# A DRAM buffer between two steps of a delta rule, laid out for its reader instead of its writer

## The chip, the cores and the metric

The kernel runs on one core of a Trainium2 chip. The metric is the device time of one execution in microseconds (us); of several runs the median is taken. Five engines work side by side: TensorE (PE in the profile, its weight loads PEld), VectorE (DVE), ScalarE (ACT), GpSimd (POOL) and SyncE (SP). SP does no arithmetic; it issues most of the DMA transfers, one after the other, and an instruction on it that waits holds back those behind it. Each engine works through its own instructions in a fixed order and waits on semaphores for the others. The data of a transfer is moved by 16 DMA engines.

## The reference

One layer of a hybrid block: an input projection feeds two branches, which are gated, projected and merged. Branch A is a gated delta rule in both directions, branch B a differential softmax attention. Sizes: 1024 latent tokens and 256 context tokens, width 1024, 8 heads of 128, all in float32. The change concerns branch A alone, and of it the inverse of a triangular matrix for each chunk of 64 tokens:

```python
a_mat = jnp.where(strict, jnp.einsum('nbhid,nbhjd->nbhij', kc * bc[..., None], kc) * decay, 0.0)
eye = jnp.eye(CHUNK, dtype=a_mat.dtype)
t_mat = lax.linalg.triangular_solve(eye + a_mat, jnp.broadcast_to(eye, a_mat.shape),
                                    left_side=True, lower=True)
u = t_mat @ (vc * bc[..., None])
w = t_mat @ (kc * (bc * jnp.exp(gc))[..., None])
```

`t_mat` feeds a scan over the chunks, one after the other, in each of the two directions. There are 1280 / 64 = 20 chunks in each direction; the kernel treats two chunks as one unit of 128 tokens and so has 10 units (NT) for each direction.

## The kernel before, in words

**Stages.** A front part normalises the tokens and computes the modulation; the input projection follows, in several parts; then comes the delta rule of the 8 heads, mixed with the rest of the projection as filling for TensorE; then the attention, mixed with the first part of the output projection; last `phase3` (from L1728), the rest of the output projections.

**What sets the order.** In the delta rule and the attention the order is planned by hand-written code. Each piece of work is a generator that yields tuples of engine, expected duration, what it depends on, and what to emit; `flow` and `turn_flow` (L70, L95) always take the next step that by these expected times can begin first, with a small handicap for each stream. The result is one fixed order for PE, DVE, ACT, POOL and SP. The expected durations stand in the source, such as 0.91 for the write and 1.82 for the read that the change touches. Outside these sections, in `phase3` too, the tile framework puts the instructions in order by itself, from estimated times of the whole program.

**The inverse of one head** (`gdn_prep`, L973 to L1132) goes by blocks of 32 x 32. A unit of 128 tokens has four diagonal blocks m = 0 to 3; with 10 units in two directions there are 2 * NT = 20 of them, u, and so 80 blocks, each with rows i and columns j.

1. TensorE forms the gram matrices, DVE scales them into `X` (L1018 to L1023). The diagonal blocks go to the DRAM buffer `da`: four transfers of the forward direction (L1034), and for the backward direction one from the tile `cb` (L1037), after a transpose on DVE.
2. *Substitution.* The 80 blocks are loaded into the tile `ab`, one block on each of 80 partitions (L1043). GpSimd clears the tile `ts` and sets its diagonal to one (L1041, L1042); `ab` and `ts` exist once, so each head uses the same ones. DVE then eliminates row by row with 31 pairs of instructions (L1048, L1050).
3. *Through DRAM.* `ts` is written to the buffer `db` (L1052), and `db` is read into `R`, one half of the tile `RR` (L1057), this time with the four blocks of a unit below each other on 128 partitions: partition 32 m + i, then the unit u and column j. The read waits on SP until the write has landed.
4. *Merge.* DVE transposes all blocks (L1058); `placed` copies blocks back into `X` on ACT (L1140) and DVE (L1139) and into `t64` (L1143), and small matmuls `pz`, `p2`, `p3` join the blocks of 32 to blocks of 64 and then 128. The result is written to `xd` (L1129).

**What else stands near it.** The scans (`scan`, L1183) load chunks of `xd` and of the masked products `qkd` (L1176); GpSimd applies the triangular mask (L1178). When a head's scan is over, `tails` normalises its output (L1280), multiplies on GpSimd (L1283), and transposes on TensorE (tile `oT`). Weights of the filling work are split in a high and a low part: ACT casts (`wh`, L765), GpSimd or DVE subtracts (`wl`, L766).

**The last stage.** `phase3` loads the eight heads' attention output `y` (L1761) through two buffers, casts each on ACT (`yh`, L1764) and subtracts on GpSimd or DVE (`yl`, L1765). A buffer is free for the next load when its `yl` is done. The weights are loaded and split in the same manner (L1725, then `wh` L1719 and `wl` L1720), and the matmuls `m` need both.

Of the kernel before, what the change touches and what calls it, by code (L numbers as in the profile page):

```python
# [8 lines left out]
F32 = mybir.dt.float32  # L9
# [14 lines left out]
NT = LT // P  # L24
NL = L // P
H = 8
# [8 lines left out]
PE, DVE, ACT, POOL, DMA, ADMA, DV2, PL1 = range(8)  # L35
# [8 lines left out]
class Block:  # L44
# [143 lines left out]
    def setup(self):  # L188
        nc, a = self.nc, self.a
        cp = self.cp = self.pool("const")  # L190
        self.dp = self.pool("spill", space=DRAM)
        ct = cp.tile([P, 3, P], F32, name="ct")
        nc.sync.dma_start(ct, a["consts"].rearrange("(a p) n -> p a n", p=P))
        self.ident, self.up, self.lo = (ct[:, i, :] for i in range(3))
        self.one = self.lo[:, 0:1]
        self.fold = cp.tile([P, P], F32, name="fold")
        nc.vector.tensor_reduce(self.fold[:, :32], self.ident.rearrange("p (a i) -> p i a", i=32), AX.X, ALU.add)
        for m in range(1, 4):
            nc.vector.tensor_copy(self.fold[:, 32 * m:32 * m + 32], self.fold[:, :32])
        self.mhalf = cp.tile([P, 1], F32, name="mhalf")  # L200
        nc.gpsimd.memset(self.mhalf, -0.5)
        self.da = self.dp.tile([H, 2 * NT, 4, 32, 32], F32, name="da")
        self.db = self.dp.tile([H, 2 * NT, 4, 32, 32], F32, name="db")
        self.ya = self.dp.tile([2, H, P, L], F32, name="ya")
        self.yb = self.dp.tile([H, P, L], F32, name="yb")
        self.gk = self.dp.tile([H, P, LT], F32, name="gk")
        self.gkk = self.dp.tile([H, P, LT], F32, name="gkk")
        self.gv = self.dp.tile([H, LT, P], F32, name="gv")
        self.gkr = self.dp.tile([H, LT, P], F32, name="gkr")
        self.rkd = self.dp.tile([H, LT], F32, name="rkd")  # L210
        self.gq = self.dp.tile([H, P, L], F32, name="gq")
        self.sza = self.dp.tile([H, P, L], F32, name="sza")
        self.szb = self.dp.tile([H, P, L], F32, name="szb")
        self.qd = self.dp.tile([2, H, P, L], F32, name="qd")
        self.kd = self.dp.tile([2, H, P, LT], F32, name="kd")
        self.vd = self.dp.tile([2, LT, H * P], F32, name="vd")
        self.gt = self.dp.tile([2 * KT, P, L], F32, name="gt")
        self.ma = self.dp.tile([KT, P, L], F32, name="ma")
        self.xd = self.dp.tile([H, P, 2, NT, P], F32, name="xd")
        self.qkd = self.dp.tile([H, P, 2, NL, P], F32, name="qkd")  # L220
        self.tbd = self.dp.tile([P, 1024], F32, name="tbd")
        self.gcd = self.dp.tile([2 * H, LT], F32, name="gcd")
        self.gad = self.dp.tile([1, D], F32, name="gad")
        self.rbd = self.dp.tile([H, L], F32, name="rbd")
        for n in ("gk", "gkk", "gv", "gq", "sza", "szb", "qd", "kd", "vd", "gt", "gcd", "ya", "yb"):
            self.dbg[n] = getattr(self, n).name
# [745 lines left out]
    def gdn_prep(self, h):  # L972
        nc, PT, V = self.nc, self.gt_, self.nc.vector  # L973
# [21 lines left out]
        for d in range(2):  # L995
            for c in range(NT):
                t = yield ACT, 0.293, [ld[d]], lambda: nc.scalar.activation(
                    X[:, d, c], X[:, d, c], AF.Abs, bias=self.gcc[:, c, d * H + h:d * H + h + 1], scale=-1.0)
# [5 lines left out]
        for c0 in range(0, NT, 2):  # L1004
# [3 lines left out]
            for j in range(2):  # L1008
                c = c0 + j
                kc = kT[:, c * P:(c + 1) * P]  # L1010
                t = yield PE, 0.2235, [tk, b], lambda: self.mm(pt[:, j * 256:j * 256 + P], kc, kc)
                if c < NL:
                    t = yield PE, 0.2235, [tk, tq, b], lambda: self.mm(pt[:, j * 256 + P:j * 256 + 256], kc, qT[:, c * P:(c + 1) * P])
# [11 lines left out]
            if c0 < NL:  # L1025
                t = yield DMA, 0.91, tQ[-2:], lambda: nc.sync.dma_start(self.qkd[h][:, :, c0:c0 + 2], qk[:, c0 // 2 % 2])
# [13 lines left out]
        ab, ts = T("ab", [80, 32, 32]), T("ts", [80, 32, 32])  # L1040
        t1 = yield PL1, 0.89, [], lambda: nc.gpsimd.memset(ts, 0.0)  # L1041
        t1 = yield PL1, 0.06, [t1], lambda: nc.gpsimd.memset(ts.rearrange("p a b -> p (a b)")[:, 0:1024:33], 1.0)  # L1042
        t = yield DMA, 0.91, st, lambda: nc.sync.dma_start(ab, self.da[h].rearrange("u m i j -> (u m) i j"))  # L1043
        tmp = T("tmp", [80, 256])
        for j in range(31):
            n, w = 31 - j, j + 1
            tv = tmp[:, :n * w].rearrange("p (a b) -> p a b", b=w)
            t = yield DV2, n * w / 960.0 + 0.08, [t, t1], lambda: V.tensor_tensor(  # L1048
                tv, ab[:, j + 1:, j:j + 1].to_broadcast([80, n, w]), ts[:, j, :w].unsqueeze(1).to_broadcast([80, n, w]), ALU.mult)
            t = yield DV2, n * w / 960.0 + 0.08, [t, t1], lambda: V.tensor_tensor(ts[:, j + 1:, :w], ts[:, j + 1:, :w], tv,  # L1050
                                                                               ALU.subtract)
        t = yield DMA, 0.91, [t], lambda: nc.sync.dma_start(self.db[h].rearrange("u m i j -> (u m) i j"), ts)  # L1052
        self.subst = h + 1
        yield lambda: self.merge == h
        RR = T("RR", [P, 2, 2 * NT, 32])
        R, Rt = RR[:, 0], RR[:, 1]
        tR = yield DMA, 1.82, [t], lambda: nc.sync.dma_start(R, self.db[h].rearrange("u m i j -> (m i) u j"))  # L1057
        tt = yield DVE, 0.735, [tR], lambda: V.transpose(Rt, R)  # L1058
        t64, tZ, placed = self.t64, [], []
        self.asides.append(self.placed(X, R, Rt, tt, tZ, placed))  # L1060
# [5 lines left out]
        for c in range(NT):  # L1066
            for (b1, b2) in ((0, 1), (2, 3)):
                t = yield PE, 0.03, [tt, b], lambda: self.mm(pz[B(b1), c], X[B(b2), 0, c, B(b1)], Rt[B(b2), c]), 0.25
                t = yield PE, 0.03, [tt, b], lambda: self.mm(pz[B(b2), c], X[B(b1), 1, c, B(b2)], R[B(b1), NT + c]), 0.25
# [7 lines left out]
        for c in range(NT):  # L1077
            for (b1, b2) in ((0, 1), (2, 3)):
                t = yield PE, 0.03, [tz, b], lambda: self.mm(p2[B(b1), c], R[B(b1), c], Z[B(b1), c]), 0.25
                t = yield PE, 0.03, [tz, b], lambda: self.mm(p2[B(b2), c], Rt[B(b2), NT + c], Z[B(b2), c]), 0.25  # L1080
# [20 lines left out]
        for c0, nb in ((5, 5), (0, 5)):  # L1101
# [4 lines left out]
            for j in range(nb):  # L1106
                c = c0 + j
                t = yield PE, 0.065, [tx, b], lambda: self.mm(pz[lo, j], X[hi, 0, c, lo], X[hi, 0, c, hi]), 0.5
                t = yield PE, 0.065, [tx, b], lambda: self.mm(pz[hi, j], X[lo, 1, c, hi], X[lo, 1, c, lo]), 0.5
# [5 lines left out]
            for j in range(nb):  # L1115
                c = c0 + j
                t = yield PE, 0.065, [tz, t6, b], lambda: self.mm(pu[lo, j], t64[lo, c], Z6[lo, c]), 0.5
                t = yield PE, 0.065, [tz, t6, b], lambda: self.mm(pu[hi, j], t64[hi, c], Z6[hi, c]), 0.5
# [5 lines left out]
            for d in range(2):  # L1124
                for c in range(c0, c0 + nb):
                    t = yield ACT, 0.263, [e, f], lambda: nc.scalar.activation(
                        X[:, d, c], X[:, d, c], AF.Copy, scale=self.beta[:, c, d * H + h:d * H + h + 1])
# [744 lines left out]
```

## Time and profile before

| | |
|---|---|
| median of 3 runs | 2076.24 us |
| runs | 2072.71, 2076.24, 2086.58 us |
| profiled execution | 2065.07 us |
| its span (first to last instruction) | 2063.3 us |
| granted TensorE clock, mean | 0.986 of full speed |
| busy: PE, DVE, ACT, POOL | 96%, 69%, 52%, 38% of the span |
| mean DMA rate | 171 GB/s |

A row of the timeline gives start and duration in us, the engine (a q behind it means its sequencer, here the issue of a transfer), the line, the operation, and out<-in by the tiles' names; in brackets stands how long the engine was idle before it, and who ended that. A row of the windows gives the stretch, its length, the busy time of PE, PEld, DVE, ACT and POOL with the number of instructions, the granted clock, the share of the 16 DMA engines that was busy, and GB/s. A row of the view of one tile gives the count, and the smallest, median and largest duration in ns. The duration of a transfer on SP is that of its issue, not of the movement; when it has landed is seen from the instruction that waits for it.

### The profile page before, as it was taken

The numbers are of one execution on the slowest core, as the hardware profiler recorded it, in microseconds if no ns is written. First come the engines' busy times: TensorE is split into PE (matmuls) and PEld (weight loads), VectorE is DVE, ScalarE is ACT, GpSimd is POOL, SyncE is SP. The second block draws the span as 40 slices with busy tenths as digits, with TensorE's granted clock in tenths as the row PEclk, the third lists the DMA queues.
The fourth block names the chain that finished last, engine by engine and source line by source line (L and its number), as shares of the span: only waits on it lengthen the run. The fifth ranks groups of instructions, "written<-read, shape, count | busy, mean of one in ns | idle before, by whom it ended". The sixth has DMA issues, their size and how long they took to land.

```text
span 2063.3 us, 38606 instructions
## 1 busy us (share of the span) xinstructions
PE 1974.1 (96%) x14207; PEld 1725.9 (84%) x14207; DVE 1423.1 (69%) x3582; ACT 1070.9 (52%) x2328; POOL 774.8 (38%) x644
## 2 busy tenths in 40 slices
PE   8999898899999999999999999999899999998999
PEld 3888677798999997887787888887788888876899
DVE  4797668866876885765665786237679899874532
ACT  4444344354234462566456654547668888773210
POOL 1213224214441331323333323334566667564122
PEclk9999999999999999999999999999999999999999
DMA  9455557545446566557754865648665575335452
GB/s 314 118 148 149 146 141 199 138 163 161 147 136 193 164 203 184 172 178 234 214 196 144 261 182 159 219 144 237 153 174 144 165 200 152 102 109 189 150 158 87
DMA packets 395840, 352.24 MB, mean 171 GB/s; under 512 B 145423, under 2 KB 344689, under 8 KB 395651
## 3 DMA queue, kind: packets, MB, share of 16 engines
q1 hardware_dynamic: 345443, 302.58, 49.9%
q10 hardware_dynamic: 50208, 47.19, 7.5%
q8 instruction: 112, 1.84, 0.4%
q14 instruction: 77, 0.63, 0.1%
HBM read 232.63 MB, written 117.08 MB: 169 GB/s over the span
## 4 chain that ended last, share of the span: by engine, by line
PE 52%; DMA 10%; DVE 8%; ACT 6%; issue 2%; SPq 1%; POOL 1%; ACTq 0%; DVEq 0%; POOLq 0%
PE mm L55 22%; PE chain L55 5%; PE mo L55 4%; PE s L55 3%; PE m L55 3%; PE v L55 3%; DVE S L1453 3%; PE ma L55 3%; PE out L55 3%; ACT S L1466 2%; PE t L58 2%; DMA hx<-in_w_in_dram 1%; PE gram L55 1%; DVE al L1527 1%; DMA sq<-gq 1%
## 5 line engine op out<-in xcount | busy, mean ns | idle before, releaser
L55 PE MATMUL mm<-hs,wh 128*128 128x512 f32 x1024 | 357.5, 413 | 0.0
L414 PE MATMUL mm<-hs,wh 128*128 128x512 f32 (+1 forms) x1024 | 291.2, 370 | 18.7 <-ACT xc L454 18.7
L55 PE MATMUL mm<-wh,hs 128*128 128x256 f32 x1472 | 274.0, 285 | 0.0
L1453 DVE TENSOR_SCALAR_CACHE_REDUCE S<-s,rsq 128x512 f32<-128x512 f32 (+1 forms) x384 | 241.8, 655 | 32.1 <-PE s L55 29.1
L414 PEld LDWEIGHTS mm<-hs,wh 128*128 128x128 f32 x1024 | 187.7, 194 | 52.8 <-ACT xc L454 22.0
L55 PEld LDWEIGHTS mm<-wh,hs 128*128 128x128 f32 x1472 | 231.3, 192 | 0.4
L1490 POOL TENSOR_TENSOR S<-S 128x1280 f32<-128x1280 f32 x64 | 188.9, 2953 | 90.1 <-ACT S L1483 87.8
L55 PE MATMUL mm<-hs,wl 128*128 128x512 f32 x512 | 213.4, 417 | 1.4 <-POOL wl L766 1.4
L55 PEld LDWEIGHTS mm<-hs,wh 128*128 128x128 f32 x1024 | 188.9, 190 | 27.0
L55 PE MATMUL mm<-wl,hs 128*128 128x256 f32 x736 | 210.2, 286 | 0.0
L1466 ACT ACTIVATE S<-S,mn 128x1280 f32<-128x1280 f32 x128 | 174.8, 1367 | 33.3 <-DVE mn L1465 32.6
L414 PE MATMUL mm<-hs,wl 128*128 128x512 f32 (+1 forms) x512 | 188.6, 368 | 0.0
L459 DVE SCALAR_TENSOR_TENSOR ac<-xc,smallT,ac 128x1284 f32<-128x1284 f32 (+1 forms) x96 | 157.0, 1635 | 11.2 <-ACT ac L455 9.0
L55 PE MATMUL s<-kk,qh 128*128 128x512 f32 (+1 forms) x384 | 145.1, 378 | 3.2 <-DVE S L1453 2.9
L55 PEld LDWEIGHTS mm<-wl,hs 128*128 128x128 f32 x736 | 141.1, 192 | 0.3
L55 PE MATMUL s<-kk,ql 128*128 128x512 f32 (+1 forms) x384 | 133.9, 359 | 0.0
L1527 DVE TENSOR_TENSOR al<-t,ah 128x512 fp32r<-128x512 f32 (+1 forms) x192 | 107.7, 593 | 10.4 <-ACT ah L1522 9.8
L414 PEld LDWEIGHTS mm<-hs,wl 128*128 128x128 f32 x512 | 99.0, 193 | 15.3
L55 PEld LDWEIGHTS mm<-hs,wl 128*128 128x128 f32 x512 | 97.7, 191 | 15.0 <-POOL wl L766 1.6
L1522 ACT CAST ah<-t 128x512 fp32r<-128x512 f32 (+1 forms) x192 | 90.0, 516 | 30.1 <-PE t L58 28.9
L1048 DVE TENSOR_TENSOR tmp<-ab,ts 80x31 f32<-80x31 f32 (+15 forms) x248 | 99.5, 401 | 8.0 <-POOL ts L1042 2.1
L58 PE MATMUL t<-ct,S 128*128 128x128 f32 x640 | 96.7, 278 | 2.8 <-POOL S L1490 1.6
(291 smaller groups left out, 5029.0 us busy)
## 6 DMA issues: line engine op xcount, KB each, us to landing
hx<-in_w_in_dram ACTq DMA_DIRECT2D x64, 256.0 KB
wr<-in_w_in_dram SPq DMA_DIRECT2D x30, 512.0 KB
X<-gcd SPq DMA_DIRECT2D x16, 640.0 KB
kd<-col SPq DMA_DIRECT2D x40, 256.0 KB
xd<-X SPq DMA_DIRECT2D x16, 640.0 KB
x<-xd SPq DMA_DIRECT2D x80, 128.0 KB
kk<-kd SPq DMA_DIRECT2D x32, 320.0 KB
wr<-in_w_in_dram ACTq DMA_DIRECT2D x18, 512.0 KB
```

The source lines that it names most:

```text
L55: self.nc.tensor.matmul(out, lhsT, rhs, start=start, stop=stop)
L58: self.nc.tensor.transpose(out, src, self.ident[:src.shape[0], :src.shape[0]])
L414: nc.tensor.matmul(pt[:, :n], wt[:, k, cs], ht[:, k, o:o + n], start=i == 0, stop=i == 3 * KT - 1)
L459: nc.vector.scalar_tensor_tensor(ac[:, w], xc[:, o + j:o + j + wd // parts], self.convw(j, ct), ac[:, w], ALU.mult, ALU.add)
L1048: t = yield DV2, n * w / 960.0 + 0.08, [t, t1], lambda: V.tensor_tensor(tv, ab[:, j + 1:, j:j + 1].to_broadcast([80, n, w]), ts[:, j, :w]. ...
L1453: e = yield DVE, 0.675 if m == 512 else 0.408, [e, self.sfree[c].get(n - 4 + c)], lambda: self.nc.vector.tensor_scalar(x["S"][c][:, o:o + ...
L1466: x["x"].append((yield ACT, 1.36, [e], lambda: nc.scalar.activation(S, S, AF.Exp, bias=x["mn"][:, c:c + 1], scale=-1.0, accum_out=w["l0"][ ...
L1490: e = yield POOL, 2.9, [e], lambda: self.nc.gpsimd.tensor_tensor(S0, S0, S1, ALU.add)
L1522: e = yield ACT, 0.48 if nb == 4 else 0.27, [t, y["old", k]], lambda: self.nc.scalar.copy(y["ah", k][:, :, q], pv)
L1527: t = yield DVE, 0.603 if k < 2 else 0.322, [e, y["old", k]], lambda: self.nc.vector.tensor_tensor(y["al", k][:, :, q], pv, y["ah", k][:, ...
```

## The change

The buffer `db` gets another order of its axes, and the two transfers are rewritten for it. Before, `db[h]` holds block after block (u, m), each of 32 x 32 numbers; after, it holds row after row (m, i) of the merged matrix, with the units u and columns j inside it. The contents and the tiles on both sides are the same.

```diff
-        self.db = self.dp.tile([H, 2 * NT, 4, 32, 32], F32, name="db")
+        self.db = self.dp.tile([H, 4, 32, 2 * NT, 32], F32, name="db")
...
-        t = yield DMA, 0.91, [t], lambda: nc.sync.dma_start(self.db[h].rearrange("u m i j -> (u m) i j"), ts)
+        t = yield DMA, 0.91, [t], lambda: nc.sync.dma_start(self.db[h].rearrange("m i u j -> u m i j"), ts)
...
-        tR = yield DMA, 1.82, [t], lambda: nc.sync.dma_start(R, self.db[h].rearrange("u m i j -> (m i) u j"))
+        tR = yield DMA, 1.82, [t], lambda: nc.sync.dma_start(R, self.db[h].rearrange("m i u j -> (m i) u j"))
```

Before, each partition of `ts` goes to one contiguous run of 4096 bytes of `db`, and the read collects runs of 128 bytes, 20 for each of 128 partitions. After, the write puts down runs of 128 bytes, 32 from each of 80 partitions, and the read takes one contiguous run of 2560 bytes for each of 128 partitions. In the compiled program the write's destination is a pattern of 20 x 128 runs of 32 numbers, its source one of 80 x 32. The order of the instructions is the same on all engines up to the last stage; there the framework's own order differs in some places on each engine.

## The prediction

> **What bounds the kernel now.** I read the page first (busy times, chain), then the time by stage, then what waits on the two transfers that change.
>
> ```profile
> PE 1974.1 (96%) x14207; PEld 1725.9 (84%) x14207; DVE 1423.1 (69%) x3582; ACT 1070.9 (52%) x2328; POOL 774.8 (38%) x644
> ...
> PE 52%; DMA 10%; DVE 8%; ACT 6%; issue 2%; SPq 1%; POOL 1%; ACTq 0%; DVEq 0%; POOLq 0%
> ```
>
> TensorE is busy 1974.1 us of a span of 2063.3, so only 89 us are idle in all, and the chain that ended last runs mostly through it. A change that touches no matmul can only make those idle stretches shorter or longer. The stages in which the changed transfers run, and the last one, whose order of instructions changes (below), look like this (length, then PE busy):
>
> ```profile
> 800.00:900.00 100.00, 94.11 (x952) 78.21 (x950) 54.51 (x164) 54.62 (x162) 29.62 (x40) 0.98 0.63 188
> 1000.00:1100.00 100.00, 91.13 (x794) 75.29 (x792) 52.60 (x152) 50.58 (x143) 31.23 (x38) 0.97 0.64 196
> 1860.00:1911.00 51.00, 47.59 (x190) 37.20 (x190) 24.85 (x21) 16.88 (x24) 23.93 (x15) 0.94 0.60 201
> ```
>
> PE idles 5.9, 8.9 and 3.4 us there. That is what can be won, and around these gaps is where something can be lost. The view of the buffer (DVE and POOL wait where "who waited" is told) says who waits for the two transfers:
>
> ```profile
> L1052 SPq DMA_DIRECT2D db<-ts x8: 320/386/578, 621.9 to 1259.4; - x8
> L1057 SPq DMA_DIRECT2D RR<-db x8: 359/378/499, 625.0 to 1263.5; - x8
> ...
>   POOL ts L1041: 46.0, 3
>   ACT X L1140: 0.2, 1
> ```
>
> This is the key. Eight writes and eight reads, and nobody but ACT, once, for 0.2 us, is seen waiting for the **read**. For the **write** GpSimd waits three times, 46.0 us in sum: its memset of `ts` for the next head may not overwrite the tile before the write has landed. The change makes the read easier, for which hardly anyone waits, and the write harder.
>
> **The change, part by part.** Each write now moves 80 rows of 4096 bytes; after, the same 320 KB as 20 x 128 = 2560 pieces of 128 bytes. Each read is now 2560 pieces of 128 bytes; after, 128 rows of 2560 bytes. No instruction is added or removed, and the planner's costs of both are as before, so the hand-planned order of the middle stands. What each takes (start, duration, engine, line; then the queue's and the first reader's rows):
>
> ```profile
> 621.89 0.34 SPq L1052 DMA_DIRECT2D db<-ts  x1
> 624.96 0.36 SPq L1057 DMA_DIRECT2D RR<-db  x1
> 629.49 1.87 ACT L1140 COPY X<-RR 32x320 f32<-32x320 f32 x4 [0.24 <-DMA RR<-db]
> ...
> 1209.73 0.38 SPq L1037 DMA_DIRECT2D da<-cb  x1
> 1212.52 0.32 SPq L1043 DMA_DIRECT2D ab<-da  x1
> ...
> 515.99 0.33 SPq L1043 DMA_DIRECT2D ab<-da  x1
> 520.89 0.20 DVE L1048 TENSOR_TENSOR tmp<-ab,ts 80x31 f32<-80x31 f32 x1
> ...
> 622.50:624.50 2.00, 2.00 (x19) 2.00 (x18) 0.69 (x1) 0.59 (x1) 0.00 (x0) 1.00 0.91 238
> 626.60:629.00 2.40, 2.40 (x22) 2.40 (x22) 1.32 (x6) 0.33 (x1) 0.00 (x0) 1.00 1.02 170
> ```
>
> *The write.* It lands in 624.96 - 621.89 = 3.07 us (the read behind it waits for that). Upper end of the new one: `da<-cb` is the one existing write of its kind, 1280 pieces of 128 bytes, landed within 1212.52 - 1209.73 = 2.79 us; twice that is 5.58, or +2.5 us. Lower end: while the scattered read runs (626.60 to 629.00) the 16 DMA engines are full, 2.40 x 1.02 x 16 = 39 us of engine time, so at most 15.3 ns for each of 2560 pieces and 2.45 us if spread evenly; the present write moves its 0.328 MB at the 238 GB/s of its window in 1.38 us; the difference is +1.1 us. A gain is excluded: same bytes, 32 times as many pieces. I take **d = +2.0 us**, nearer to `da<-cb`, the only row of a scattered write.
>
> Two statements of the Trainium skill's page "DMA: Bandwidth & Descriptors" speak against the change. "Specifications" says that transfers under 512 bytes fall below line rate and are read, modified and written back; the row of `da<-cb` above does not show such a surcharge over the read's 15.3 ns, since 2.79 us hold its whole round trip. "Why a DMA increments its semaphore by 16 and not by 1" says that a transfer runs on the largest number of engines up to 16 that divides the outermost size on both sides; these are 80 and 20 after the change, so 10 engines, and the write would take 2560 x 15.3 ns / 10 = 3.9 us, d = +2.5 and a sum of +8.5, an estimate by that page. No row of before can show it.
>
> *The read.* It now takes 629.49 - 624.96 = 4.53 us to the first reader. The nearest contiguous load of 320 KB, `ab<-da`, took 520.89 - 515.99 = 4.90 to its first reader (no gain); by the engine time above it would save 2.45 - 1.38 = 1.1 us. I take -0.7.
>
> *Where d meets TensorE.* The three waits of GpSimd, what stands behind them on its queue, and who waits for that:
>
> ```profile
> 625.00 0.95 POOL L1041 MEMSET ts<- 80x1024 f32 x1 [12.95 <-DMA db<-ts]
> 626.28 0.20 DVE L1048 TENSOR_TENSOR tmp<-ab,ts 80x31 f32<-80x31 f32 x1 [2.06 <-POOL ts L1042]
> ...
> 812.07 0.95 POOL L1041 MEMSET ts<- 80x1024 f32 x1 [25.39 <-DMA db<-ts]
> 814.73 1.26 POOL L766 TENSOR_TENSOR wl<-hx,wh 128x512 fp32r<-128x512 f32 x1
> 816.05 0.50 PE L55 MATMUL mm<-hs,wl 128*128 128x512 f32 x1 [1.40 <-POOL wl L766]
> ...
> 1011.90 0.95 POOL L1041 MEMSET ts<- 80x1024 f32 x1 [7.68 <-DMA db<-ts]
> 1012.82 1.90 POOL L1283 TENSOR_TENSOR oa<-oa,of 128x1024 f32<-128x1024 f32 x1
> 1014.77 0.66 PE L58 MATMUL oT<-ct,oa 128*128 128x128 f32 x4 [1.82 <-POOL oa L1283]
> ```
>
> After head 0's write DVE starts the next substitution later by d, but TensorE shows no wait in that stretch, so 0. After head 2's write GpSimd's masks and the weight split `wl` come later and TensorE, already waiting 1.40 us for `wl`, waits **2.0** more. After head 4's write the same happens through `oa`, which TensorE awaits for 1.82 us already: **+2.0**. Both queues run in a fixed order, so nothing steps in.
>
> *Where the pair write + read meets TensorE.* Where SP goes straight from write to read (heads 0, 1, 7) the read lands later by 2.0 - 0.7 = 1.3 us.
>
> ```profile
> 630.41 0.83 DVE L1058 STREAM_TRANSPOSE RR<-RR 128x640 f32<-128x640 f32 x1
> ...
> 672.51 0.50 SPq L1057 DMA_DIRECT2D RR<-db  x1
> 688.73 0.84 DVE L1058 STREAM_TRANSPOSE RR<-RR 128x640 f32<-128x640 f32 x1
> ...
> 1263.48 0.37 SPq L1057 DMA_DIRECT2D RR<-db  x1
> 1268.72 0.83 DVE L1058 STREAM_TRANSPOSE RR<-RR 128x640 f32<-128x640 f32 x1
> ...
> 806.93 0.58 SPq L1052 DMA_DIRECT2D db<-ts  x1
> 813.20 0.42 SPq L1057 DMA_DIRECT2D RR<-db  x1
> ```
>
> Head 0: the transpose starts 630.41 - 629.49 = 0.9 us after the data, so 0.4 us late. Head 1: 16 us from issue to transpose, 0. Head 7: 1268.72 - 1263.48 - 4.53 = 0.7 us of slack, so 0.6 us late. In heads 2 to 6 SP reaches the read no sooner than 6.27 us after the write (head 2, the shortest), more than the new 5.07, so the read is not held and only gets shorter, for nobody. SP itself is blocked longer in heads 0, 1 and 7 by d; behind it stand prefetches of later chunks, 0.
>
> *The tail.* The last stage is put in order automatically, from estimated times, and the compiled order of the changed kernel differs there. The matmuls are the same but interleaved otherwise; on ACT the second weight cast (L1719) now stands ahead of the first two `yh` casts (L1764), on GpSimd the second `wl` ahead of the first `yl`, on SP a weight load ahead of the second pair of `y` loads.
>
> ```profile
> 1867.84 2.01 ACT L1764 CAST yh<-y 128x1024 fp32r<-128x1024 f32 x2
> 1872.23 1.15 ACT L1719 CAST wh<-wr 128x512 fp32r<-128x512 f32 x2 [2.38 <-PE ma L55]
> ...
> 1873.45 2.00 POOL L1720 TENSOR_TENSOR wl<-wr,wh 128x512 fp32r<-128x512 f32 x1 [1.17 <-ACT wh L1719]
> ...
> 1874.31 0.79 SPq L1761 DMA_DIRECT2D y<-yb  x2
> ...
> 1892.91 0.80 SPq L1761 DMA_DIRECT2D y<-yb  x2
> ...
> 1891.86 0.51 PE L55 MATMUL m<-yl,wh 128*128 128x512 f32 x1 [1.56 <-POOL yl L1765]
> 1900.67 0.50 PE L55 MATMUL m<-yl,wh 128*128 128x512 f32 x1 [1.04 <-POOL yl L1765]
> ```
>
> The second weight cast waits for TensorE until 1872.23, so the `yh` casts move from 1867.84 to 1873.4, the first `yl` behind the second `wl` to 1875.45, its end to 1877.9; the second `y` pair, which needs the freed buffer, goes from 1874.31 to 1877.9 (+3.6). The later pairs had slack between them; following cast, split, load and landing with the same durations I get the last pair at 1894.4 instead of 1892.91: **+1.5 us** on the waits for `yl`. Ends: both waits vanish (-2.6), or the whole +3.6 arrives.
>
> Sum: 2.0 + 2.0 + 0.4 + 0.6 + 1.5 = **+6.5 us**; with d open, 2d + (d - 1.6) + (d - 1.4) + 1.5. The profiled execution took 2065.07 us (span 2063.3), so 2071.6 for one like it; the median of before is 2076.24 (2072.71 to 2086.58), 11 us above that execution, and I predict 2076.24 + 6.5 = **2082.7**.
>
> **Rivals.**
> 1. *The write is hidden as well, or the tail falls well.* If fixed latency dominates, d is near 0, since 3.07 us contain 1.38 of moving; then the middle adds nothing and the tail gives -2.6 to +1.5: 2073.6 to 2077.7. For: the read's wait is 0.2 us, and even the scattered read lands in 4.53. Against: GpSimd's two waits have no slack at all, so any d above zero shows.
> 2. *Slower by over 1%: the scattered write lands so late that GpSimd's memset stalls the fixed order.* The place is L1041 and L1057, the price d per exposed head. The formula 4d - 3.0 + 1.5 passes 20.8 us (1% of the median) at d = 5.6, a landing of 8.7 us. Pieces at twice 15.3 ns on 10 of the 16 engines would take 7.8 us instead of 1.38, d = 6.4: +24.1, 2100. For: the split of a 20-row pattern is shown by no row. Against: `da<-cb` writes just such pieces, and for d = 5.6 it would have to be slower than twice that row by 3.1 us.
> (By the Trainium skill's two statements cited above, the second alone stays in the forecast, the two together are this rival.)
> 3. *Faster by over 1%.* It would need the read's landing to gate TensorE, which 0.2 us of waits excludes.
>
> **How the numbers follow.** Forecast (d from 1.1 to 2.5 with the tail's ends: 2075.7 to 2086.8) 0.65; rival 1 0.22; rival 2 0.11; rival 3 0.02. 1%, about 21 us, is also about what a measurement of this kernel can tell from no change, given 14 us between its three runs. Forecast and rival 1 fall within 1%: 0.87. Range: the cases' ends 2073.6 and 2086.8, widened by the spread of the runs shown (-4, +10): 2069 to 2097.
>
> **What would show it.** In the profile after: GpSimd's three waits for `db<-ts` longer by about 2 us each; TensorE's waits at `wl` (L766) and `oT` near 816 and 1015 grown from 1.40 and 1.82 to 3 or 4 us; from write to read on SP about 5 us where it was 3.07; the read's first reader after about 3.8 us; the last `y` pair later by 1 to 2 us after the stage's start. I am wrong if the write still lands in about 3 us (rival 1), or in 9 or more (rival 2), or if the last stage's idle PE time leaves 1 to 7 us.

## The result, and the profile after

The changed kernel takes **2090.07 us** (median of 11 runs, 2084.15 to 2098.38) against **2071.47 us** before (median of 11 runs, 2064.53 to 2086.58): a ratio of **1.0093, 95% interval 1.0073 to 1.0113**, about 19 us slower. The profiled execution took 2094.96 us, 4.9 above its median, where that of before lay 6.4 below its own; so 11 of the 30 us between the two profiles are spread between runs. Below, effects are taken from ratios and given in us of 2071.

The busy times of the page, then what waits on the two transfers, after:

```profile
PE 1984.1 (95%) x14207; PEld 1734.4 (83%) x14207; DVE 1424.1 (68%) x3582; ACT 1070.6 (51%) x2328; POOL 774.9 (37%) x644
```

```profile
L1052 SPq DMA_DIRECT2D db<-ts x8: 797/808/877, 624.8 to 1283.5; - x8
L1057 SPq DMA_DIRECT2D RR<-db x8: 323/404/478, 630.9 to 1289.7; - x8
...
  POOL ts L1041: 51.5, 3
  ACT X L1140: 3.7, 2
```

The other engines do the same work in the same time. TensorE idles 2093.2 - 1984.1 = 109.1 us, 20 more than before, and its busy time is 10 us longer for the same 14207 matmuls (on that the last section). GpSimd's memset waits 5.5 us longer. The issue of the write itself takes SP 0.81 us where it took 0.39.

What TensorE waits for from 600 to 1350 us, the stretch of the eight heads (us in total, times, longest), before and then after:

```profile
PE chain L55 <- ACT vd L1214: 7.8, 3, 4.3
PE chain L55 <- DMA vv<-gv: 3.5, 2, 2.8
PE chain L55 <- DMA x<-xd: 3.2, 1, 3.2
PE oT L58 <- POOL oa L1283: 1.8, 1, 1.8
PE mm L55 <- POOL wl L766: 1.4, 1, 1.4
PE chain L55 <- ACT vn L1218: 0.9, 1, 0.9
```

```profile
PE chain L55 <- ACT vd L1214: 9.0, 4, 3.5
PE oT L58 <- POOL oa L1283: 6.9, 1, 6.9
PE chain L55 <- ACT vn L1218: 5.0, 1, 5.0
PE mm L55 <- POOL wl L766: 4.3, 1, 4.3
PE chain L55 <- DMA x<-xd: 3.9, 2, 2.0
```

Two of the grown waits are those of the prediction: `oT`, from 1.8 to 6.9, and `wl`, from 1.4 to 4.3. A third, `vn`, is not: it belongs to the scan and grew from 0.9 to 5.0. The timeline of head 3 shows where it comes from. First SP's issues before:

```profile
868.79 0.32 SPq L1052 DMA_DIRECT2D db<-ts  x1
870.65 0.32 SPq L1289 DMA_DIRECT2D sz<-sza  x1
...
875.55 0.32 SPq L1176 DMA_DIRECT2D x<-xd  x1
```

and after, with what follows on ScalarE and TensorE:

```profile
877.19 0.80 SPq L1052 DMA_DIRECT2D db<-ts  x1
879.03 6.08 SPq L1289 DMA_DIRECT2D sz<-sza  x1
...
887.34 0.62 SPq L1176 DMA_DIRECT2D x<-xd  x1
...
896.67 0.37 ACT L1214 ACTIVATE vd<-chain,edk 128x128 f32<-128x128 f32 x1 [1.67 <-DMA x<-xd]
...
896.94 0.26 ACT L1218 COPY vn<-chain 128x128 f32<-128x128 f32 x1
...
897.25 1.23 PE L55 MATMUL chain<-vd,kk 128*128 128x128 f32 x4 [4.99 <-ACT vn L1218]
```

The load `sz` behind the write needs 6.08 us to be *issued*, where it needed 0.32. The profile names no engine that it waits for; that the write's pieces fill the queue is a reading, which the experiments test. The scan's next chunk, `x<-xd`, is requested 887.34 - 877.19 = 10.2 us behind the write instead of 875.55 - 868.79 = 6.8, arrives late, and TensorE waits 4.99 us (this is the whole wait for `vn`). The same hold shows in six heads: the first transfer behind the write takes 4.08, 2.40, 2.19, 6.08, 3.31 and 3.66 us in heads 0 to 5, 21.7 us in sum, where these six took 2.1 us before.

### The profile page after: what moved, and what is told of

Same layout as the page of the kernel before. It is cut to its first block, busy times and chain, and to the rows that moved or that the text cites. A ratio compares the mean times of both kernels' runs of the same rounds, so it can differ in the third digit from the quotient of the medians.

```text
span 2093.2 us, 38605 instructions
## 1 busy us (share of the span) xinstructions
PE 1984.1 (95%) x14207; PEld 1734.4 (83%) x14207; DVE 1424.1 (68%) x3582; ACT 1070.6 (51%) x2328; POOL 774.9 (37%) x644
## 5 line engine op out<-in xcount | busy, mean ns | idle before, releaser
L1048 DVE TENSOR_TENSOR tmp<-ab,ts 80x31 f32<-80x31 f32 (+15 forms) x248 | 100.5, 405 | 11.4 <-DMA ab<-da 5.8
L1227 DVE SCALAR_TENSOR_TENSOR S<-S,egl,chain 128x128 f32<-128x128 f32 x128 | 43.2, 345 | 92.9 <-PE chain L55 89.6
```

The lines of the kernel that those rows point to most:

```text
L1227: t = yield DVE, 0.263, [t], lambda: V.scalar_tensor_tensor(Sn, S, self.egl[:, c, g:g + 1], pc[:, 2], ALU.mult, ALU.add)
```

## The experiments

Three accounts stood against each other. **M**: the write lands late, GpSimd's memset waits for it, and `wl` and `oa` behind it hold TensorE (the prediction's largest terms). **Q**: the write holds SP's queue, and the transfers behind it come late. **The rest**: the new read, or the other order in the last stage. Line numbers of variants differ by up to three from those above.

**Which of the two transfers.** The first two kernels complete a square: write contiguous or scattered, read contiguous or scattered. `contig_both`:

```diff
-self.db[h].rearrange("m i u j -> u m i j"), ts)
+self.db[h].rearrange("m i u j -> (m i u j)").rearrange("(p f) -> p f", p=80).rearrange("p (i j) -> p i j", i=32), ts)
```

> Contiguous write (80 rows of 4 KB) and contiguous read; the relayout between them is left out, so the merge works on permuted blocks. Theory A (the scattered write costs the time, the contiguous read gains a little): 2067 to 2073 us against 2071.5 of before, the write landing after about 3 us as before, the read about 1 us earlier than the scattered one, and the transfer behind the write issued in 0.4 us. Theory B (the time comes from the other order of instructions in the last stage, or from anything in the new read): it keeps most of the loss, 2083 to 2090 us.

`scatter_both` (from the changed kernel):

```diff
-nc.sync.dma_start(R, self.db[h].rearrange("m i u j -> (m i) u j"))
+nc.sync.dma_start(R, self.db[h].rearrange("m i u j -> (m i u j)").rearrange("(u p j) -> p u j", p=P, j=32))
```

> Write scattered as after, and the read scattered too (2560 pieces of 128 bytes on each side); the relayout is left out, so the merge works on permuted blocks. Theory A: the loss of the write (19 us over before) stays whole and the gain of the contiguous read goes: 2090 to 2096 us, the wait of POOL's memset about 51 us as in after. Theory B: near before, 2071 to 2078 us.

| write | read | ratio to before (95%) | median us |
|---|---|---|---|
| contiguous | scattered (before) | 1 | 2071 |
| contiguous | contiguous | 0.9995 (0.9978 to 1.0013) | 2070.91 |
| scattered | scattered | 1.0103 (1.0078 to 1.0129) | 2092.09 |
| scattered | contiguous (after) | 1.0093 (1.0073 to 1.0113) | 2090.07 |

The scattered write costs 20 to 21 us, whichever way the read goes; the contiguous read gains 0.05 to 0.1%, less than can be measured. `contig_both` has the last stage in the changed kernel's order, so that order costs nothing measurable either. The rest falls.

**How the pieces are spread, and how many.** The write goes to other addresses, over 16 or 5 engines, and in half as many pieces:

```diff
-self.db[h].rearrange("m i u j -> u m i j"), ts)
+self.db[h].rearrange("m i u j -> (m i u j)").rearrange("(b a j) -> a b j", a=16, j=32), ts)
```

with `a=16` in `lanes16`, `a=5` in `lanes5`, and `a=16, j=64` in `half_pieces`. The traces have 16 semaphore increments from the landing of each write of `lanes16` and 5 for those of `lanes5`.

> As after, with the same 2560 pieces of 128 bytes written to other addresses so that they go over 16 DMA engines (160 each) and not 10 (256 each); the relayout is left out. Theory A1 (the few engines make the write late): the write lands 1.2 to 2 us earlier per head than in after, and a half to two thirds of the loss goes: 2075 to 2082 us. Theory A2 (the number of small pieces, however spread, or their being writes): as after within 4 us, 2086 to 2094 us, with the next transfer on SP held 2 to 6 us in its issue as in after.

> As after, with the same 2560 pieces of 128 bytes over 5 DMA engines (512 each, about 3.3 us more per head at 13 ns a piece); the relayout is left out. Theory A1 (engines): the write lands about 3 to 4 us later than after's, and the loss grows by 4 to 5 heads times that: 2103 to 2118 us, with POOL's memset waiting about 10 to 20 us more in all. Theory A2 (the number of small pieces decides, not the engines): 2086 to 2096 us.

> Write to other addresses in 1280 pieces of 256 bytes over 16 engines (against 2560 pieces of 128 bytes over 16 in lanes16, which took 2089.0 us), read contiguous; the relayout is left out. If the number of pieces sets both the hold of SP and the landing: half of lanes16's loss of 18 us goes, 2076 to 2082 us, and the transfer behind the write is held about half as long. If a write whose two sides differ in shape costs this in any case: 2085 to 2092 us.

| write | pieces per engine | six issues behind it, us | ratio (95%) | loss, us |
|---|---|---|---|---|
| `contig_both` | | 2.1 | 0.9995 (0.9978 to 1.0013) | -1 |
| `half_pieces`, 1280 x 256 B, 16 engines | 80 | 4.4 | 1.0033 (1.0014 to 1.0052) | 7 |
| `lanes16`, 2560 x 128 B, 16 engines | 160 | 15.8 | 1.0081 (1.0056 to 1.0107) | 17 |
| after, 2560 x 128 B, 10 engines | 256 | 21.7 | 1.0093 (1.0073 to 1.0113) | 19 |
| `lanes5`, 2560 x 128 B, 5 engines | 512 | 37.9 | 1.0186 (1.0157 to 1.0214) | 39 |

The third column is the sum of the durations of the first SP issue behind the write in heads 0 to 5; in head 3 that is `sz`, here of `half_pieces`, `lanes16` and `lanes5`:

```profile
874.62 1.80 SPq L1289 DMA_DIRECT2D sz<-sza  x1
```

```profile
869.38 4.55 SPq L1289 DMA_DIRECT2D sz<-sza  x1
```

```profile
882.51 7.42 SPq L1289 DMA_DIRECT2D sz<-sza  x1
```

The loss follows the hold: over `contig_both` the hold grows by 2.3, 13.7, 19.6 and 35.8 us, the loss by about 8, 18, 20 and 40. For `half_pieces` the loss is well above the hold. For `lanes16` both expectations missed in part: the write does land earlier than in after, as A1 said (below), but only about 2 us of the loss go, as A2 said. `lanes5` came out as A1 had it. `half_pieces` has the time that the account of the pieces gave, though its hold fell to a sixth of that of `lanes16`, and not to half. This is a correlation, though: landing and hold grow together here.

**Taking account M away.** One tile `ts` for all heads, cleared for head 0 alone, in before's layout and in the changed one:

```diff
-        ab, ts = T("ab", [80, 32, 32]), T("ts", [80, 32, 32])
-        t1 = yield PL1, 0.89, [], lambda: nc.gpsimd.memset(ts, 0.0)
+        ab = T("ab", [80, 32, 32])
+        if not h:
+            self.ts = T("ts", [80, 32, 32])
+        ts = self.ts
+        t1 = yield PL1, 0.89, [], lambda: h or nc.gpsimd.memset(ts, 0.0)
```

and likewise for the second memset.

> Before's layout, one tile ts for all heads, its two memsets done for head 0 alone (left out for heads 1 to 7, so their substitution starts from the rows of the head before): nothing on POOL waits for the write any more. Theory M (the loss of the change reaches TensorE through the memset that waits for the write, POOL's wl and oa behind it): TensorE's waits for oa L1283 and wl L766 (1.8 and 1.4 us in before) go, 2066 to 2071 us against 2071. Theory Q (the loss comes through SP's queue, which the write with 2560 pieces holds): the same 2066 to 2071 us here; the pair with the next run tells them apart.

> The changed layout with the same memsets left out. Theory M: TensorE's waits for oa L1283 (6.9 us) and wl L766 (4.3 us) go, and nearly all of the loss with them: 2069 to 2076 us, at most 5 over before_nomemset. Theory Q: only the part of POOL goes (8 us of waits), and 8 to 14 us over before_nomemset stay: 2077 to 2084 us, TensorE still waiting about 5 us for vn L1218 in head 5, and transfers behind the write still held 2 to 6 us.

Measured: 1.0005 (0.9986 to 1.0024) and 1.0086 (1.0060 to 1.0112), medians 2076.05 and 2091.38 beside a before of 2073.74. With no memset waiting for the write, 0.81% of the change's 0.93% are still there (0.5 to 1.1%, with both intervals). **Account M does not carry the loss.** TensorE's waits in the changed layout without the memsets, 600 to 1350 us:

```profile
PE chain L55 <- ACT vn L1221: 7.9, 2, 4.6
PE chain L55 <- ACT vd L1217: 7.3, 4, 3.6
PE chain L55 <- DMA x<-xd: 5.7, 2, 3.7
```

The 6.9 and 4.3 us for `oa` and `wl` are gone, and the scan's waits for `vn` and `x<-xd` have grown in their place. Account Q's waits were there behind the others. It had expected some 8 us less, and the time has not fallen by them. The profile shows where they went: TensorE idles 2092.9 - 1990.7 = 102.2 us, 7 less than after, but is busy 1990.7 us instead of 1984.1, at a granted clock of 0.979 instead of 0.982. So that the memset's waits have no part at all in the loss is not shown.

**Moving the write off SP.** `act_write`:

```diff
-lambda: nc.sync.dma_start(self.db[h].rearrange("m i u j -> u m i j"), ts)
+lambda: nc.scalar.dma_start(self.db[h].rearrange("m i u j -> u m i j"), ts)
```

> The changed kernel with the write issued from ScalarE's queue and not SP's, so that the loads behind it on SP aren't held by it; layout, pieces, memset and the read on SP stay. ScalarE now waits in its own order for the end of the substitution and pays about 0.8 us for each issue. Theory Q: SP's loads are issued in 0.3 to 0.6 us again, the wait for vn L1218 in head 5 falls from 5.0 to about 1 us, and 6 to 12 us of the loss go, less what ScalarE loses: 2078 to 2086 us. Theory M: the write lands no earlier, the memset waits as in after (about 50 us in all), 2088 to 2096 us.

Measured: 1.0103 (1.0079 to 1.0128), 2095.28 us, no gain. By the numbers expected that speaks for M, and the run before speaks against it. SP's waits for the write, after and then in `act_write`:

```profile
SPq L1057 <- DMA db<-ts: 6.7, 2, 5.4
```

```profile
SPq L1057 <- DMA db<-ts: 21.9, 4, 7.0
SPq L1176 <- DMA db<-ts: 8.2, 1, 8.2
```

SP is no longer held in an issue, but it now waits for the write at the read, 21.9 us instead of 6.7, and 8.2 us ahead of a load of the scan. TensorE's waits from 600 to 1350 us changed too:

```profile
PE pz L55 <- DVE RR L1058: 3.8, 1, 3.8
PE mm L55 <- ACT zo L917: 3.7, 1, 3.7
...
PE chain L55 <- ACT vn L1218: 1.6, 1, 1.6
```

The wait for `vn` fell from 5.0 to 1.6 us, as Q expected, and `wl` is gone from the list. In their place stand waits for the merged blocks (`pz`, 1.4 in after), for `zo` on ScalarE, which now issues the write (none in after), and for `fin` (3.2 us instead of 0.5). The loss has moved to other places. Which of them keeps the time up was not tested, so taking the hold off SP has not been shown to win anything back, and this run decides nothing between hold and landing.

**Holding SP without a scattered write.** To before's kernel, two transfers of 512 bytes are added, the second waiting for the first, so that SP stands still for some microseconds:

```diff
+        self.hz = self.dp.tile([H, 2, P], F32, name="hz")
+        self.held = lambda h: [nc.sync.dma_start(self.hz[h, i:i + 1], self.hz[h, i - 1:i] if i else self.a["consts"][0:1]) for i in range(2)]
...
-lambda: nc.sync.dma_start(self.db[h].rearrange("u m i j -> (u m) i j"), ts)
+lambda: (nc.sync.dma_start(self.db[h].rearrange("u m i j -> (u m) i j"), ts), self.held(h))
```

This is `hold_write1`; in `hold_read1` the same stands behind the read (L1057), in `hold_ahead` just ahead of the read.

> Before's layout, write and read as they were; right behind each write, SP issues two transfers of 512 bytes from DRAM to DRAM, the second waiting for the first (about 2 to 3.5 us in which SP issues nothing else; 16 tiny transfers in all, the write itself lands no later). Theory Q (what costs is that the transfers queued behind the write on SP come 2 to 6 us later, whatever holds them): most of the change's loss appears without the scattered write, 2083 to 2094 us. Theory L (what costs is the late landing of the scattered pieces or their load on the DMA engines): 2071 to 2077 us.

> The same two tiny transfers right behind each read instead of behind the write. Theory Q with the place that decides (few transfers stand closely behind the read, which is why before's scattered read could hold SP's next transfer 1.2 to 1.6 us at no price): 2071 to 2079 us, at most half of what the hold behind the write costs. If any hold of SP costs the same: as hold_write1. Theory L: 2071 to 2077 us.

> Before's layout with the same two tiny transfers put ahead of each read: the loads that stand on SP between write and read come as early as in before, the read and what follows it come about 3 us later. If the late loads between write and read carry the cost (hold_write1 delayed them and the read, and took 18 us more; hold_read1 delayed only what follows the read, and took none): 2071 to 2079 us. If it is the late read: 2083 to 2094 us.

| two tiny transfers | ratio to before (95%) | median us (before beside it) | us |
|---|---|---|---|
| behind the write | 1.0079 (1.0053 to 1.0105) | 2092.52 (2074.63) | +16 |
| ahead of the read | 1.0028 (1.0012 to 1.0045) | 2082.20 (2075.64) | +6 |
| behind the read | 0.9995 (0.9979 to 1.0011) | 2073.17 (2074.63) | -1 |

Head 3 of `hold_write1`, TensorE's largest waits in it, and GpSimd's wait for the write:

```profile
877.24 0.32 SPq L1054 DMA_DIRECT2D db<-ts  x1
877.92 0.56 SPq L205 DMA_DIRECT2D hz<-in_consts_dram  x1
883.65 0.51 SPq L205 DMA_DIRECT2D hz<-hz  x1
884.26 0.53 SPq L1291 DMA_DIRECT2D sz<-sza  x1
```

```profile
PE chain L55 <- DMA x<-xd: 6.9, 2, 4.8
PE chain L55 <- ACT vd L1216: 4.2, 2, 2.5
PE chain L55 <- ACT vn L1220: 4.1, 1, 4.1
```

```profile
  POOL ts L1043: 42.7, 3
```

`sz` is requested 884.26 - 877.24 = 7.0 us behind the write, 5.2 later than before's 870.65 - 868.79 = 1.9, and TensorE waits for the scan's `x` and `vn` as after does. In sum over heads 0 to 5, the issue of the first of before's own transfers behind the write ends 22 us later than in before; in after it is 20. The write is the contiguous one, GpSimd's waits for it are no longer than before (42.7 us against 46.0), and yet 16 of the 19 us appear. The same two transfers behind the read are free. **Account Q is shown in this direction**: a hold of that length behind the write makes most of the loss without a scattered write. The reverse, the scattered write without the hold, no run reached (`act_write` moved the waits).

`hold_ahead` came out between its two expectations, and its hold is longer than meant: over the eight heads the read is issued 36 us later behind its write than in before, where it is 18 in `hold_write1` and 14 in after. Its 6 us are therefore rather an upper end for what the late read costs, and the rest of the 16, some 10 us or more, is left for the loads that stand between write and read. This is a difference of two runs and takes the two parts as adding up. How the remaining 3 us divide among landing, memset and last stage was not separated; nor was each load tried by itself.

## Why the prediction was right, and where it was wrong

The time lies in the range, and its ratio of 0.93% below the 1% that was given as bound, though the interval reaches past it (1.13%). But the sum behind it was +6.5 us where +19 were measured, and 2090.07 lies above the forecast case's own ends (2075.7 to 2086.8; by the formula given, the lower one comes to 2075.0): it is in the range only because that was widened by the spread of the runs. That 2082.7 comes as near as it does is luck too: it stood on a median of 2076.24 of three runs; eleven give 2071.47, and the same sum from there gives 2078.0.

The write's landing after, heads 0, 2 and 7:

```profile
624.82 0.88 SPq L1052 DMA_DIRECT2D db<-ts  x1
...
630.79 0.95 POOL L1041 MEMSET ts<- 80x1024 f32 x1 [15.82 <-DMA db<-ts]
...
819.72 0.95 POOL L1041 MEMSET ts<- 80x1024 f32 x1 [25.48 <-DMA db<-ts]
...
1283.50 0.80 SPq L1052 DMA_DIRECT2D db<-ts  x1
1289.72 0.32 SPq L1057 DMA_DIRECT2D RR<-db  x1
```

- *What bounds the kernel*: right in part. Of the 30 us between the two profiles 20 are idle TensorE. The other 10 are longer busy time, though the prediction said that a change without matmuls can only move the idle stretches. The read's gain is worth nothing, as said.
- *The write's landing, d = +2.0 (1.1 to 2.5)*: about right. In head 0 it lands in 630.79 - 624.82 = 5.97 us against 625.00 - 621.89 = 3.11, in head 7 in 6.22 against 4.05: 2.9, above the upper end, and 2.2. In head 2 it is 1.8. GpSimd's three waits grew by 5.5 us in sum where 6 were said. The trace has ten semaphore increments from the landing of each write, so ten engines.
- *The read, -0.7*: in head 0 its first reader starts 4.6 us after the issue, as before; in the other seven heads its last increment comes 0.5 to 2.3 us sooner behind the issue (in head 7 2.85 us instead of 3.97). A gain on which nothing hung.
- *Heads 2 and 4, +2.0 each*: `wl` grew by 2.9 and `oT` by 5.1, so the places were seen rightly, though `oT` grew by more than twice what was said. That these waits make the time was wrong: without the memset they are gone and the loss stays (0.81%), with the scan's waits grown in their place.
- *"SP itself is blocked longer in heads 0, 1 and 7 by d; behind it stand prefetches of later chunks, 0."* **This is the step that failed.** SP is held in heads 0 to 5, not by a wait but in the issue of the next transfer, 2.2 to 6.1 us each, and its loads are not far ahead of their use: the hold alone, without the rest of the change, costs 16 us. I had taken the 0.3 to 0.4 us of an issue as given, whatever stands ahead of it.
- *The read in heads 2 to 6 is not held*, since SP reaches it 6.27 us or more after the write: true, and it gave away the point, for SP reaches it so late because of the loads between, which are what gets late. Nor does SP go straight from write to read in heads 0 and 1, as was said: before, `ab<-da` is issued between them at 622.28 and `hx<-tbd` at 669.96.
- *The tail, +1.5*: TensorE's waits for `yl` and `yh` grew from 2.6 to 6.2 us, to the upper end (+3.6). But in `contig_both`, which has the same order, they are 5.3, and it takes no longer than before.
- *Rival 2* had the direction right and the place wrong: not the memset on GpSimd, but SP's queue.

By the Trainium skill's page "DMA: Bandwidth & Descriptors", section "Why a DMA increments its semaphore by 16 and not by 1", ten engines carry the write, and the trace agrees with its ten increments. By the section "Specifications" of the same page of the Trainium skill, transfers under 512 bytes are read, modified and written back. Head 7 shows how long a piece takes. In `lanes16` and `lanes5` the read follows its write by:

```profile
1269.34 0.61 SPq L1052 DMA_DIRECT2D db<-ts  x1
1274.43 0.32 SPq L1057 DMA_DIRECT2D RR<-db  x1
```

```profile
1294.40 0.77 SPq L1052 DMA_DIRECT2D db<-ts  x1
1303.53 0.33 SPq L1057 DMA_DIRECT2D RR<-db  x1
```

that is 5.09 us at 160 pieces for each engine, 6.22 at 256 (after) and 9.13 at 512: 11.8 and 11.4 ns a piece, less than the 15.3 ns that the prediction took for a piece of the scattered read. So these runs show no surcharge for short writes over the pieces of the read.

## What to carry to other kernels

A relayout through DRAM has to scatter on one side; put the scattered transfer where little stands behind it on its queue, and not where the loads of the next stage are queued. Moving it to ScalarE's queue gained nothing here, so another queue has to be tried and not assumed. When a transfer gets many small pieces, look at the issues behind it, not only at who waits for its data. And a wait seen in the trace is not yet its price: taken away, another may stand right behind it, so test a hold by itself, with tiny dependent transfers at the place in question.

## What the runs showed of the hardware

**A transfer of 2560 pieces held the next issue of its queue.** In heads 0 to 5 of after this issue took 2.2 to 6.1 us (median 3.5), against 0.3 to 0.4 behind 80 rows of 4 KB. It is no matter of writing: behind the scattered read of `hold_read1` the tiny `hz` took 1.64 to 5.52 us to be issued:

```profile
L205 SPq DMA_DIRECT2D hz<-in_consts_dram x8: 1639/3159/5522, 627.3 to 1268.7; - x8
```

In `hold_write1`, behind the contiguous write, the same instruction took 0.55 to 0.60. Before's scattered read held its successor too: in heads 1, 3 and 6 that issue took 1.2 to 1.6 us. That was free: in `contig_both` these issues take 0.3 to 0.5 us, and the time is the same.

**TensorE's granted clock fell at some of its waits, and not at all of them.** In head 0, where TensorE waits for the late blocks, the rows of the changed kernel are (length, PE busy, the granted clock in the third column from the end):

```profile
645.00:650.00 5.00, 3.02 (x40) 2.62 (x40) 4.83 (x7) 2.05 (x2) 3.10 (x3) 0.97 0.60 189
650.00:660.00 10.00, 10.00 (x99) 9.68 (x97) 5.62 (x12) 4.60 (x14) 0.72 (x2) 0.84 0.30 107
```

Ten fully busy microseconds run at 0.84 behind 2 idle ones; before, without the gap, the same ten ran at 1.00:

```profile
650.00:660.00 10.00, 10.00 (x111) 9.73 (x108) 7.84 (x19) 5.06 (x14) 0.72 (x2) 1.00 0.51 185
```

Yet where TensorE waits 3.52 us for `vd`, until 1115.61, the clock then stays at 1.00:

```profile
1115.00:1120.00 5.00, 4.39 (x97) 3.49 (x97) 3.27 (x7) 4.08 (x12) 1.27 (x1) 1.00 0.01 4
```

The mean clock was 0.977 to 0.983 in the runs of after and 0.979 to 0.988 in those of before beside the variants. Of the 30 us between the two profiles, 20 are idle time and 10 are longer busy time, and 1974.1 x 0.986 / 0.982 = 1982 accounts for 8 of these. In two other runs idle and busy time grow together as well: `hold_write1` idles 17 us more than before and is busy 15 longer, `after_nomemset` idles 13 more and is busy 17 longer, at 0.981 and 0.979. So a wait may cost more than its length. That the added idle time brings the clock down was not tried by itself.
